# Single-bank gate and up products, and state-space scan blocks with one exponential, summed feature-major by TensorE

## The chip, the cores and the metric

The kernel runs on one core of a Trainium2 chip as one launch. The metric is the device time in microseconds (us), taken as the median of three runs, and lower is better. Engines are named as in the profile: PE is TensorE's matmul (PEld its weight load), DVE is VectorE, ACT is ScalarE, POOL is GpSimd, and SP is the queue that issues most of the DMAs.

## What is computed

Two layers of an encoder over 1024 tokens of width 1024. Each layer has one input projection, four mixers (latent attention "mla", a long convolution "hyena", windowed attention "swa", a state-space scan "ssd"), a norm and an output projection, a gated feed-forward, and a gated per-layer embedding. The change touches the scan and the first half of the feed-forward. Cut to those:

```python
D_MODEL = 1024; SEQ = 1024; D_FF = 2816; SSD_HEADS = 4; SSD_HEAD_DIM = 64; SSD_GROUPS = 2; SSD_CHUNK = 128
...
    a_cs = jnp.cumsum(A, axis=-1)
    seg = a_cs[..., :, None] - a_cs[..., None, :]
    lmat = jnp.exp(jnp.where(tril, seg, -jnp.inf))
    cb = jnp.einsum('bctgn,bcsgn->bgcts', Cc, Bc)
    y_diag = jnp.einsum('bgcts,bgrcts,bcsgrp->bctgrp', cb, lmat, X)
...
    y_off = jnp.einsum('bctgn,cbgrpn,bgrct->bctgrp', Cc, prev, jnp.exp(a_cs))
...
    y = y_f + y_b + dsum * xs            # forward scan, backward scan, skip
...
        y_d = ssd_mixer(...) * jax.nn.silu(ssd_z)
...
        gate = dwconv_centred(h @ ffn_w_gate[i], ffn_conv_w[i], ffn_conv_b[i])
        f = (jax.nn.silu(gate) * (h @ ffn_w_up[i])) @ ffn_w_down[i]
```

## The kernel before

All of a program's engines work from one list of operations. Generators write the list (`interleave` mixes several flows by shares, `stagger` starts a flow's next item one step behind the last), and a scheduler then sets each engine's order by its own simulated timeline, so the order on an engine is not always that of the text. An engine works through its own list in order: an operation that waits holds up all behind it on that engine.

**PSUM.** Results of matmuls land in PSUM, here in two pools: `one()` gives one of four single-bank tiles of 128x512 (named "ps" in the profile), `two()` one of two tiles of two banks, 128x1024 (named "pp"). Together they are eight banks.

**The scan stage.** In each layer `ssd`, `swa` and `mla_keys` are interleaved (402 to 531 us in layer 0 of the profiled execution, 1978 to 2107 us in layer 1). `ssd` cuts the tokens into 8 chunks of 128 and the four heads into 2 groups. `states(c, g)` makes the chunk's state: two transposes, `xt` on ACT, `xd` on DVE, one matmul, and the running `prev`. `output(c, g)`, 16 times in a layer, makes the result: on PE a mask matmul of 512 columns (L880) and 8 matmuls of 128 columns (L885) that put the log decays into one bank; on ACT four exponentials of 128x128, each with its own bias column `lg`, give `Lm`; on PE the two products of C with B and with `prev` into bank `pc`; on DVE `wt` (two steps) and `yo`; on POOL the sum of the two directions of `yo`; on PE a transpose of that sum (L906) and the product of `wt` with `xt`; on ACT a copy `yt` of the transpose; on DVE two additions of 64x128 that write y over B's own buffer (named "xbc<-ps,yt"). After all outputs, z and xs are read from DRAM again, DVE adds `dsum` times xs and DVE and POOL multiply by z (L923 to L927), and y is stored. Seven of the eight "X" buffers of 8 KB per partition are in use by then. `mla_keys` takes four of them for its `kT` in the stage's second half, as the scan gives them back.

**Gate and up.** `gate_up` (about 780 to 1245 us in layer 0, 2350 to 2815 us in layer 1) makes both products of the feed-forward for 22 blocks of 128 features by a two-by-two scheme with 7 products in place of 8. One product is 12 matmuls of 512 columns in one bank: 4 blocks of the inner dimension, times three because an operand is split into a high and a low part (`split`: ACT writes the high part, POOL or DVE the rest, L84 and L87). For a feature the two weights come by DMA into the two `wraw` buffers (`load`, L1372), DVE and POOL form sums and differences (`s`, and `wraw` over itself), five parts are split into the ring "H" of 8, and the products are read out of PSUM by DVE with an addition (to `u`, `v`, `g`) or by ACT (to `v`). Two pairs of products share a two-bank tile: the products with t2 and t1 (`pa`), and those with t4 and 22 (`pb`). The first product of the next features runs in `first`, the convolution and SiLU of a feature in `gated`, and its stores in `paired`. The first features' `first` runs ahead of the loop (`starts`). All these matmuls show as line L99, in `mm`; DVE's and POOL's additions as L87, ACT's work as L84, DVE's multiply-adds as L90.

## Time and profile before

| what | value |
|---|---|
| time, median of 3 runs | 3204.69 us (3196.22 to 3207.54) |
| profiled execution, own time | 3194.46 us |
| its span, first to last instruction | 3192.7 us |
| mean granted clock of TensorE in it | 0.970 |
| busy PE, DVE, POOL, ACT | 2946.4, 2440.4, 1771.2, 1291.6 us |
| as a share of the span | 92%, 76%, 55%, 40% |
| scan stages | 402 to 531 us, 1978 to 2107 us |
| feature loops of gate and up | about 818 to 1245 us, 2385 to 2815 us |

A busy share is time with an instruction at work; matmuls are pipelined and their ends are modelled, so the step from one matmul's start to the next one's start is a better measure of what it costs than its duration. A timeline's row gives start, duration, engine, line, operation, what is written and read, and how many instructions of one kind are put together; in square brackets stand the idle time ahead of it on its engine and what ended it. A granted clock of 1.00 is TensorE's level of 2.4 GHz, and 0.50 that of 1.2 GHz. The profiled execution lies 10.2 us (0.3%) under the median of the runs.

### The profile page before, as it was taken

The page shows a single profiled execution, that of the slowest core. Times are in us where ns is not written, and L with a number is a line of the kernel's source. Part 1 is how long each engine was busy: PE and PEld are TensorE (multiplying, and loading weights), DVE is VectorE, ACT ScalarE, POOL GpSimd, SP SyncE. Part 2 cuts the span into 40 slices and gives each one's busy share as a digit, 9 for nine tenths or more (in the row PEclk, how much of TensorE's full clock was granted, in tenths as well). Part 3 has the DMA queues.
Part 4 walks back from the last instruction along what each step waited for, and adds up shares of the span by engine and source line. Part 5 has one row for each costly group of instructions (what it writes and reads, how often), then busy time and mean ns, then how long its engine had stood idle before and what let it go on. Part 6 is the DMA issues. An engine that isn't in the chain of part 4 may idle for free.

```text
span 3192.7 us, 40546 instructions
## 1 busy us (share of the span) xinstructions
PE 2946.4 (92%) x14316; PEld 2420.9 (76%) x14316; DVE 2440.4 (76%) x3711; ACT 1291.6 (40%) x2278; POOL 1771.2 (55%) x1371
## 2 busy tenths in 40 slices
PE   6999988999899999999989998889989999999996
PEld 4887866877678777787867877768767787777785
DVE  7678786878766777889777786868786677768986
ACT  4332365743333334443342333667333333344341
POOL 5455533527555666887435463335185556679845
PEclk9999998999999999999999998999999999999998
DMA  5466523022233326523335664130322333274332
GB/s 181 152 202 213 180 85 137 16 84 86 76 99 106 102 96 225 189 93 124 114 107 159 219 215 158 53 122 17 107 73 83 99 111 99 101 257 146 106 132 89
DMA packets 153427, 400.44 MB, mean 125 GB/s; under 512 B 16578, under 2 KB 43462, under 8 KB 152968
## 3 DMA queue, kind: packets, MB, share of 16 engines
q1 hardware_dynamic: 138968, 347.18, 32.5%
q0 software_dynamic: 14256, 50.67, 5.2%
q8 instruction: 114, 1.87, 0.2%
q14 instruction: 89, 0.73, 0.1%
HBM read 294.50 MB, written 103.28 MB: 125 GB/s over the span
## 4 chain that ended last, share of the span: by engine, by line
PE 48%; DVE 22%; POOL 9%; DMA 8%; issue 8%; ACT 5%; SPq 0%; DVEq 0%; POOLq 0%; ACTq 0%
PE ps L99 17%; PE pp L99 15%; PE ps L1613 7%; DMA wraw<-in_ffn_w_gate_dram 4%; POOL H L87 2%; DVE g L90 2%; DVE u L87 2%; PE ps L942 2%; DVE w L87 2%; POOL w L87 2%; DVE H L90 2%; PE ps L1054 1%; DVE v L87 1%; ACT w L84 1%; POOL wraw L87 1%
## 5 line engine op out<-in xcount | busy, mean ns | idle before, releaser
L99 PE MATMUL pp<-x,wh 128*128 128x512 f32 x1344 | 430.0, 398 | 1.8 <-ACT wh L84 1.8
L1613 PE MATMUL ps<-part 128*128 128x512 f32 x1440 | 341.4, 393 | 14.7 <-DVE H L87 6.1
L87 POOL TENSOR_TENSOR w<-wraw,w 128x512 fp32r<-128x512 f32 x164 | 232.7, 1431 | 206.0 <-ACT w L84 205.8
L1613 PEld LDWEIGHTS ps<-part 128*128 128x128 f32 x1440 | 270.8, 189 | 78.4 <-DVE H L87 9.8
L99 PEld LDWEIGHTS pp<-x,wh 128*128 128x128 f32 x1344 | 256.1, 193 | 54.2 <-ACT wh L84 2.0
L99 PE MATMUL ps<-x,w 128*128 128x512 f32 x1056 | 261.6, 395 | 10.8 <-ACT v L84 10.8
L99 PE MATMUL pp<-x,w 128*128 128x512 f32 x1056 | 258.3, 394 | 14.1 <-DVE v L87 9.7
L99 PE MATMUL pp<-x,wl 128*128 128x512 f32 x672 | 266.8, 397 | 3.8 <-POOL wl L87 3.8
L99 PE MATMUL pp<-xq,w 128*128 128x512 f32 x1056 | 264.4, 392 | 5.8 <-DVE x L87 4.5
L84 ACT ACTIVATE w<-wraw 128x512 fp32r<-128x512 f32 x264 | 152.8, 622 | 267.6 <-DMA wraw<-in_ffn_w_up_dram 169.9
L87 POOL TENSOR_TENSOR wl<-wraw,wh 128x1024 fp32r<-128x1024 f32 (+2 forms) x61 | 153.6, 2520 | 173.6 <-ACT wh L84 119.8
L99 PEld LDWEIGHTS pp<-x,w 128*128 128x128 f32 x1056 | 196.9, 188 | 63.7 <-DVE v L87 13.8
L87 POOL TENSOR_TENSOR part<-fr,part 128x512 fp32r<-128x512 f32 x140 | 220.5, 1602 | 43.7 <-ACT part L84 43.4
L99 PEld LDWEIGHTS ps<-x,w 128*128 128x128 f32 x1056 | 199.0, 190 | 59.9 <-ACT v L84 18.0
L99 PEld LDWEIGHTS pp<-xq,w 128*128 128x128 f32 x1056 | 198.0, 188 | 51.2 <-ACT w L84 5.1
L99 PE MATMUL ps<-wo,yn 128*128 128x512 f32 x768 | 188.0, 401 | 5.5 <-DVE H L90 3.1
L87 DVE TENSOR_TENSOR part<-wr,part 128x512 fp32r<-128x512 f32 x124 | 155.5, 1278 | 39.0 <-ACT part L84 38.7
L1039 POOL TENSOR_TENSOR P<-P,smr 128x1024 f32<-128x1024 f32 x64 | 121.2, 1895 | 110.1 <-DVE smr L1038 101.2
L99 PEld LDWEIGHTS ps<-wo,yn 128*128 128x128 f32 x768 | 145.4, 193 | 39.6 <-DVE H L90 5.4
L99 PE MATMUL ps<-wh,x 128*128 128x512 f32 x512 | 158.7, 390 | 0.0
L99 PEld LDWEIGHTS pp<-x,wl 128*128 128x128 f32 x672 | 129.1, 192 | 30.6 <-POOL wl L87 4.7
L90 DVE SCALAR_TENSOR_TENSOR g<-g,pp 128x1023 f32<-128x1023 f32 x88 | 128.4, 1460 | 27.0 <-ACT g L84 25.6
(385 smaller groups left out, 7264.5 us busy)
## 6 DMA issues: line engine op xcount, KB each, us to landing
fr<-fp SPq DMA_DIRECT2D x70, 512.0 KB, 3.7
c_fwd<-in_c_fwd_dram POOLq DMA_DIRECT2D x64, 512.0 KB, 5.4
wraw<-in_ffn_w_up_dram SPq DMA_DIRECT2D x50, 512.0 KB, 3.5
fp<-u SPq DMA_DIRECT2D x100, 256.0 KB, 2.4
wraw<-in_ffn_w_gate_dram SPq DMA_DIRECT2D x44, 512.0 KB, 3.8
wraw<-in_w_in_dram SPq DMA_DIRECT2D x42, 512.0 KB, 3.7
wr<-in_ffn_w_down_dram SPq DMA_DIRECT2D x36, 512.0 KB, 4.8
c_inv<-in_c_inv_dram POOLq DMA_DIRECT2D x32, 512.0 KB, 4.8
```

The lines of the kernel that those rows point to most:

```text
L84: self.nc.scalar.activation(out, in_, func, **kw)
L87: (eng or self.nc.vector).tensor_tensor(out, a, b, op=op)
L90: return self.nc.vector.scalar_tensor_tensor(out, a, s, b, op0=op0, op1=op1)
L99: ins = self.nc.tensor.matmul(out, a, b, start=i == 0, stop=i == n - 1)
L942: ins = self.nc.tensor.matmul(out[0:64] if j else out, v[:, 0, :] if j else v.rearrange("p i d -> p (i d)"), terms[i][1 + j], start=k == 0 ...
L1039: nc.gpsimd.tensor_tensor(P, P, sm.to_broadcast([128, T]), op=ALU.mult)
L1054: nc.tensor.transpose(pt[:, j * 128:(j + 1) * 128], P[:, c0:c0 + 128], self.ident)
L1613: nc.tensor.matmul(ps, u, v, start=k == 0 and (p != 1 or ch == 0), stop=k == 5 and (p != 1 or ch == last))
```

## The change

Gate and up: around the feature loop the pool of two-bank tiles is closed and a pool of four single-bank tiles ("pt") opened in its place (`swap2`), and products go in turn to "pt" and "ps", so a product never shares a tile; at the loop's end the pool is set back. The scan: `lg` is split in two parts (`lgs`), and two matmuls of 512 columns add it to the log decays in PSUM, so that one exponential of 128x512 without a bias makes all of `Lm`. The skip term becomes a matmul of xs with a diagonal matrix (`skip`), the `wt` product is made as two halves of 64 columns, and the two directions of `yo` are added by two matmuls with the identity, all into the same 128 columns of `py`. DVE's one last step multiplies that by z and writes y. For that z is read into an eighth X buffer, `zs`, as the stage begins. The POOL sum, the transpose, the ACT copy, the two additions, the second reading of xs and z and the last passes over all of y go away.

```diff
+    def swap2(self, name, bufs):
+
+        self.st2.close()
+        self.ps2 = self.st2.enter_context(self.tc.tile_pool(name=name, bufs=bufs, space=PSUM, reuse_waits="tile"))
 
...
+        zs = self.xp.tile([128, 2, T], F32, name="zs", tag="X")
+        for g in range(2):
+            nc.sync.dma_start(zs[:, g], zd[:, g])
+        sk = self.pool(ss, f"sk{l}")
+        skip = sk.tile([128, 2, 128], F32, name="skip")
+        for g in range(2):
+            self.act(skip[:, g], self.ident, scale=dsum[:, g:g + 1])
+        lgs = [sk.tile([128, 8, 8], F32R, name=f"lg{i}") for i in range(2)]
+        self.split(*lgs, lg)
...
+            for a in lgs:
+                nc.tensor.matmul(bv, self.identr, jv(a, c, g, 128), start=False, stop=False)
             for d in range(2):
                 for h in range(2):
                     j = d * 4 + g * 2 + h
@@ -885,10 +903,7 @@
                         nc.tensor.matmul(bv[:, d, h, :], a[:, c, j:j + 1].to_broadcast([128, 128]), self.tri[:, d, :],
                                          start=False, stop=a is Al and d + h == 2)
             yield
-            for d in range(2):
-                for h in range(2):
-                    j = d * 4 + g * 2 + h
-                    self.act(Lm[:, d, h, :], bv[:, d, h, :], AF.Exp, bias=lg[:, c, j:j + 1])
+            self.act(Lm, bv, AF.Exp)
...
-            yo = s2.tile([128, 2, 2, 64], F32, name="yo", bufs=3)
-            self.tt(yo, pc[:, 256:512].rearrange("p (d h x) -> p d h x", d=2, h=2), jv(eacs, c, g, 64), ALU.mult)
+            yo = s2.tile([128, 2, 128], F32, name="yo", bufs=3)
+            self.tt(yo.rearrange("p d (h x) -> p d h x", h=2), pc[:, 256:512].rearrange("p (d h x) -> p d h x", d=2, h=2),
+                    jv(eacs, c, g, 64), ALU.mult)
             self.tt(wt, wt, pc[:, 0:128].unsqueeze(1).to_broadcast([128, 2, 128]), ALU.mult)
             yield
-            self.tt(yo[:, 0], yo[:, 0], yo[:, 1], ALU.add, nc.gpsimd)
-            yield
-            py = self.one()
-            nc.tensor.transpose(py[:, 256:384], yo[:, 0].rearrange("p h x -> p (h x)"), self.ident)
-            yield
-            yt = s2.tile([128, 128], F32, name="yt", bufs=3)
-            self.act(yt, py[:, 256:384])
-            self.mm(py[:, 0:256], [(xt[g][:, c, 0], wt.rearrange("p h t -> p (h t)"))])
-            yield
-            y = res[1, g]
+
+            py = self.one()[:, 0:128]
+            nc.tensor.matmul(py, skip[:, g], res[0, g][:, cs], start=True, stop=False)
             for h in range(2):
                 hs = slice(h * 64, h * 64 + 64)
-                self.tt(y[hs, cs], py[hs, h * 128:h * 128 + 128], yt[hs], ALU.add)
+                nc.tensor.matmul(py[hs], xt[g][:, c, 0, hs], wt[:, h], start=False, stop=False)
+            for d in range(2):
+                nc.tensor.matmul(py, yo[:, d], self.ident, start=False, stop=d == 1)
+            yield
+            self.tt(res[1, g][:, cs], py, zs[:, g, cs], ALU.mult)
...
-        for g in range(2):
-            nc.sync.dma_start(res[2, g], zd[:, g, :])
-            x = self.wp.tile([128, T], F32, name="wraw", tag="wraw", bufs=2)
-            nc.sync.dma_start(x, xbc[0][:, g])
-            self.stt(res[1, g], x, dsum[:, g:g + 1], res[1, g], ALU.mult, ALU.add)
-            self.tt(res[1, g], res[1, g], res[2, g], ALU.mult, nc.gpsimd if g else nc.vector)
-        yield
...
-            def product(w, b, ps=None):
-                ps = self.one() if ps is None else ps
+            def product(w, b):
+                if next(turn):
+                    ps = self.ps2.tile([128, 512], F32, name="pt", tag="pt")
+                else:
+                    ps = self.one()
...
-                lo, hi = slice(0, 512), slice(512, 1024)
-                pa = self.two()
                 u = small()
-                self.tt(u, product(w2, B["t2"], pa[:, lo]), v1, add)
+                self.tt(u, product(w2, B["t2"]), v1, add)
                 u4 = small()
-                self.tt(u4, product(w1, B["t1"], pa[:, hi]), u, add)
+                self.tt(u4, product(w1, B["t1"]), u, add)
...
-                pb = self.two()
-                self.tt(g[:, 0:512], product(w22, B["t4"], pb[:, lo]), u, add)
+                self.tt(g[:, 0:512], product(w22, B["t4"]), u, add)
                 c12 = fu.tile([128, 512], F32, name="u", tag="u", bufs=6)
-                self.tt(c12, product(w4, B["22"], pb[:, hi]), u4, add)
+                self.tt(c12, product(w4, B["22"]), u4, add)
...
+            turn = itertools.repeat(0)
...
+            turn = itertools.cycle((1, 0))
+            self.swap2(f"ps3_{l}", 4)
             for f in range(NF):
                 last = feature(f, last, starts[f] if f < 3 else None)
             gated(*last)
...
```

On PE, in layer 0's feature loop, the first matmul of each product of one feature before (x_7021 and x_7023 are the operands of `first` and its second step, xq_7624, x_7622, xq_7626, xq_7628 and x_7620 those of t2, t1, t3, t4 and 22):

```order
L99 MATMUL pp_9169<-xq_7624,w2_9156 128x512 [waits DVE_49]
L99 MATMUL pp_9095<-x_7620,w2_9022 128x512 [waits DVE_49]
L99 MATMUL ps_9359<-xq_7626,w2_9308 128x512 [waits Activation_49]
L99 MATMUL pp_9169<-x_7622,w2_9151 128x512 [waits DVE_49]
L99 MATMUL pp_9244<-xq_7628,w2_9162 128x512 [waits DVE_49]
L99 MATMUL ps_9374<-x_7023,w2_9295 128x512 [waits DVE_49]
L99 MATMUL ps_9425<-x_7021,w2_9422 128x512 [waits Activation_49]
```

and after (x_6993 and x_6995, then xq_7596, x_7594, xq_7598, xq_7600 and x_7592 in the same roles):

```order
L100 MATMUL pt_9911<-xq_7596,w2_9897 128x512 [waits Activation_49]
L100 MATMUL ps_9926<-x_7594,w2_9892 128x512 [waits DVE_49]
L100 MATMUL pt_9952<-xq_7598,w2_9900 128x512 [waits DVE_49]
L100 MATMUL ps_9967<-x_6995,w2_9887 128x512 [waits DVE_49]
L100 MATMUL pt_9981<-xq_7600,w2_9903 128x512 [waits DVE_49,Activation_49]
L100 MATMUL ps_9996<-x_7592,w2_9907 128x512 [waits DVE_49,Activation_49]
L100 MATMUL pt_10019<-x_6993,w2_10016 128x512 [waits DVE_49,Activation_49]
```

Before, the halves of a tile stand apart, with products of the neighbouring feature and of "ps" between them; after, a feature's products stand in the order of the text, one bank each, and a bank comes up again eight products later.

On PE, in the scan stage of layer 0, from one output to the next before:

```order
L906 MATMUL ps_4464<-ident_116,yo_4370 128x128 [waits PE_49,Activation_49,Pool_49]
L99 MATMUL ps_4414<-wt_4306,xt_3562 128x256 [waits Activation_49]
L99 MATMUL ps_4470<-xbc_3555,xbc_3552 128x128 [waits PE_49,Activation_49]
L99 MATMUL ps_4470<-prev_3563,xbc_3555 128x256
L99 MATMUL ps_4464<-wt_4347,xt_3562 128x256 [waits Activation_49]
L880 MATMUL ps_4479<-mask_130,identr_132 128x512 [waits DVE_49,PE_49]
L885 MATMUL ps_4479<-tri_128,s_Ah_612 128x128
```

and after:

```order
L921 MATMUL ps_4469<-xbc_3549,skip_3571 128x128 [waits Activation_49]
L924 MATMUL ps_4469<-wt_4388,xt_3564 64x128 x2
L926 MATMUL ps_4469<-ident_116,yo_4427 128x128 x2
L100 MATMUL ps_4478<-xbc_3555,xbc_3552 128x128 [waits DVE_49]
L100 MATMUL ps_4478<-prev_3563,xbc_3555 128x256
L896 MATMUL ps_4484<-mask_130,identr_132 128x512 [waits DVE_49,PE_49]
L898 MATMUL ps_4484<-lg0_3574,identr_132 128x512
L898 MATMUL ps_4484<-lg1_3575,identr_132 128x512
L903 MATMUL ps_4484<-tri_128,s_Ah_612 128x128
```

An output's last part, two pieces before with POOL and ACT between them, is one piece after, with three waiting matmuls in a round in place of four.

On SP, as the scan stage begins, before:

```order
L612 DMA z0_271<-cv_3476 128x1024 [waits DMAHW6_49,Activation_49]
L826 DMA xbc_3549<-xs0_276 128x1024 [waits DMAHW7_49,PE_49]
L826 DMA xbc_3555<-cs0_278 128x1024 [waits DMAHW4_49]
L1105 DMA wraw_4249<-sk0_273 64x1024 [waits DMAHW5_49,DVE_49]
L612 DMA z0_271<-cv_3534 128x1024 [waits DMAHW7_49,Activation_49]
L1108 DMA wraw_4254<-sq0_272 128x1024 [waits DMAHW0_49,PE_49]
```

and after:

```order
L619 DMA z0_271<-cv_3476 128x1024 [waits DMAHW5_49,Activation_49]
L833 DMA xbc_3549<-xs0_276 128x1024 [waits DMAHW7_49,PE_49]
L833 DMA xbc_3555<-cs0_278 128x1024 [waits DMAHW4_49]
L842 DMA zs_3565<-z0_271 128x1024 [waits DMAHW5_49,PE_49]
L1111 DMA wraw_4262<-sk0_273 64x1024 [waits DMAHW6_49,DVE_49]
L1114 DMA wraw_4267<-sq0_272 128x1024 [waits DMAHW0_49,PE_49]
L619 DMA z0_271<-cv_3534 128x1024 [waits DMAHW1_49,Activation_49]
L842 DMA zs_3565<-z0_271 128x1024 [waits DMAHW2_49,DMAHW1_49]
```

The two halves of z, 512 KB each, are read in here, the first ahead of swa's keys; rows of the same load are left out.

## Rows read from the trace of the kernel before

**Rows 1.** Windows, gate and up, layer 0: PE, PEld, DVE, ACT, POOL busy, clock, DMA, GB/s.

```profile
835.00:1235.00 400.00, 389.33 (x1683) 314.34 (x1682) 293.56 (x326) 139.03 (x205) 230.81 (x163) 1.00 0.33 108
```

**Rows 2.** Waits of PE, feature loop of layer 0: total us, times, longest.

```profile
PE pp L99 <- DVE v L87: 4.8, 4, 1.6
...
PE pp L99 <- DVE g L87: 2.3, 3, 1.3
```

**Rows 3.** Waits of PE, feature loop of layer 1, the longest sum.

```profile
PE pp L99 <- DVE v L87: 5.4, 5, 1.6
```

**Rows 4.** Timeline of all engines, layer 0, around one wait of PE.

```profile
1137.26 2.89 PE L99 MATMUL ps<-x,w 128*128 128x512 f32 x12
...
1139.99 2.91 PE L99 MATMUL pp<-xq,w 128*128 128x512 f32 x12
...
1142.89 0.69 DVE L87 TENSOR_TENSOR s<-wraw 128x512 f32<-128x512 f32 x1 [3.01 <-DMA wraw<-in_ffn_w_gate_dram]
...
1144.24 3.03 PE L99 MATMUL pp<-x,w 128*128 128x512 f32 x12 [1.34 <-DVE g L87]
...
1144.38 1.57 POOL L87 TENSOR_TENSOR w<-s,w 128x512 fp32r<-128x512 f32 x1 [1.66 <-ACT w L84]
...
1147.11 2.91 PE L99 MATMUL ps<-xq,w 128*128 128x512 f32 x12
```

**Rows 5.** Windows, the scan stage of both layers, and 22 us of layer 0's.

```profile
402.00:531.00 129.00, 112.56 (x621) 86.85 (x622) 97.71 (x325) 81.43 (x249) 44.99 (x45) 0.93 0.23 70
1978.00:2107.00 129.00, 110.86 (x619) 84.82 (x619) 96.97 (x325) 81.94 (x250) 44.98 (x46) 0.93 0.24 73
479.00:501.00 22.00, 20.46 (x113) 17.48 (x114) 14.11 (x37) 9.10 (x35) 6.00 (x9) 0.84 0.21 67
```

**Rows 6.** Waits of PE, scan stage of layer 0.

```profile
PE ps L99 <- DVE xd L87: 8.8, 4, 3.8
PE ps L99 <- DVE xbc L87: 2.0, 1, 2.0
PE ps L99 <- ACT Lm L84: 1.5, 3, 0.7
```

**Rows 7.** Timeline of PE, scan stage of layer 1, two outputs.

```profile
2061.22 0.49 PE L99 MATMUL ps<-xbc 128*128 128x128 f32 x2 [0.72 <-ACT Lm L84]
...
2061.55 0.60 PE L99 MATMUL ps<-prev,xbc 128*128 128x256 f32 x2
...
2061.98 0.59 PE L99 MATMUL ps<-wt,xt 128*128 128x256 f32 x2
...
2062.23 0.58 PE L880 MATMUL ps<-mask,identr 128*128 128x512 f32 x1
...
2062.65 0.22 PE L885 MATMUL ps<-tri,s_Ah 128*128 128x128 f32 x1
...
2063.49 0.30 PE L906 MATMUL ps<-ident,yo 128*128 128x128 f32 x1
...
2066.89 0.49 PE L99 MATMUL ps<-xbc 128*128 128x128 f32 x2 [0.67 <-ACT Lm L84]
```

**Rows 8.** Groups by form, scan stage of layer 0: busy us, mean ns, idle before.

```profile
L84 ACT ACTIVATE Lm<-ps,s_lg 128x128 f32<-128x128 f32 x64 | 18.3, 368 | 16.3 <-PE ps L885 16.3
...
L87 DVE TENSOR_TENSOR xbc<-ps,yt 64x128 f32<-64x128 f32 x32 | 9.1, 286 | 1.7 <-PE ps L99 1.3
```

**Rows 9.** Timeline of PE, scan stage of layer 0, around 64-column products.

```profile
516.97 0.40 PE L99 MATMUL ps<-wh,ck 128*128 128x512 f32 x1
517.30 1.51 PE L99 MATMUL ps<-wpt,sV 128*64 128x256 f32 x6
518.74 0.88 PE L1149 MATMUL pp<-ident,ws 128*128 128x128 f32 x6
519.45 0.60 PE L99 MATMUL ps<-wt,xt 128*128 128x256 f32 x2
```

**Rows 10.** Timeline of PE, end of layer 0's scan stage.

```profile
535.06 0.69 PE L99 MATMUL ps<-wh,cn 128*128 128x384 f32 x1 [3.60 <-ACT cn L84]
```

More of the change, by code (lines that the diff above doesn't have):

```diff
@@ L1 @@
+import itertools
 import math
@@ L231, in build @@
         self.ps1 = self.pool(ctx, "ps1", 4, space=PSUM)
-        self.ps2 = self.pool(ctx, "ps2", 2, space=PSUM)
+        self.st2 = ctx.enter_context(ExitStack())
+        self.ps2 = self.pool(self.st2, "ps2", 2, space=PSUM)
         self.dram = self.pool(ctx, "dram", 1, space=DRAM)
@@ L1490, in gate_up @@
             gated(*last)
+            self.swap2(f"ps2_{l}", 2)
     def down(self, l, fd, hmid, H, end, ed):
```

## The prediction

> **What bounds the kernel now.** I began with the busy shares in the table: PE is at work for 92% of the span and no other engine passes 76%, so a stage is shorter only where PE waits less or computes less. The windows over the two stages that the diff touches come next. In gate and up PE is busy 389.33 of 400 us at a granted clock of 1.00, DVE 293.56, POOL 230.81 [rows 1]: PE's own stage, with at most 10.7 us to be had from 400 in each layer. The list of PE's waits says who holds it: DVE, by reading a product of a two-bank tile to `v` (4.8 us in 4 waits) or `g` (2.3 us in 3) [rows 2]; in layer 1 the reading to `v` alone is 5.4 us in 5 waits [rows 3].
>
> The timeline shows how such a wait comes about [rows 4]. DVE stands until 1142.89 for the gate weight's DMA (idle 3.01 us), makes `s`, and only then reads the finished product to `g`; PE, whose next product goes to the other half of that tile, starts it at 1144.24 after 1.34 us of idling. Two products follow each other by 2.73 us when nothing stalls (1137.26 to 1139.99), by 2.87 behind a wait (1144.24 to 1147.11), so a wait costs 0.14 us more than its length.
>
> In the scan stage PE is busy 112.56 of 129 us in layer 0 and 110.86 in layer 1, at a mean clock of 0.93 [rows 5]. Its waits there are mostly for `xd` (8.8 us in 4), which DVE makes late because its buffer waits for DMAs as the stage begins; 2.0 us is for the last addition of y ("xbc"), and 1.5 us for `Lm` [rows 6].
>
> **Gate and up, part by part.** The change removes no product; it gives each its own bank and lets a bank rest for seven products. What it can remove are the waits for a half tile's reader: 4.8 + 2.3 in layer 0 [rows 2], 5.4 [rows 3] plus an estimated 2.3 for `g` in layer 1, 14.8 us in all in some 15 waits, and 15 x 0.14 = 2.1 us of refill: 17 us. Not all comes back, since the operands are nearly as late. In the example the next product's operand, `w` from `s`, is finished by POOL at 1144.38 + 1.57 = 1145.95 [rows 4]. Without the wait PE would have asked for it at 1147.11 - 1.34 = 1145.77, so 0.18 of 1.34 us would stay, about a seventh. I take 15 us of 17. The ends are nothing, if DMA and splits set the pace at once, and 2 x 10.7 = 21 us, the whole idle time. Before the loop the pool change waits for the last two-bank tiles' readers, and after it `down` waits for the last products' readers; I cost both at zero, since such a reading is one DVE step of 0.68 us and half the banks are not affected, and keep 2 us a layer as the upper end (each change can expose one wait like the 1.34 us and its refill).
>
> **The scan, part by part.** Steps between starts give PE's prices [rows 7]. A 256-column product in full precision takes 0.43 us (2061.55 to 2061.98), so one of 128 columns 0.22. The mask matmul of 512 columns takes 2062.65 - (2061.98 + 0.43) = 0.24. The eight decay matmuls take 0.84 (2062.65 to 2063.49), and by their step a one-pass transpose of 128 columns about 0.11. An output gains two 512-column matmuls (0.48) and the skip product (0.22), and two identity products replace one transpose (0.43 - 0.11 = 0.32); the two halves of the `wt` product cost what the whole did. That is 1.02 us, 16.3 us for the 16 outputs of a layer, on the engine that is the bound. The 64-column halves add a change of shape. Around six products of 64 columns, from 516.97 to 519.45, PE takes 2.48 us [rows 9] where 0.23 + 6 x 0.23 + 6 x 0.11 = 2.27 would do: 0.2 for going in and out, 3.4 us a layer for 16 pairs. Its lower end is nothing, if the gap was a load of weights that the new order hides. One rule of the Trainium skill speaks against the change here: "TensorEngine Tiling (Array Packing)", Key Properties, says that a change of tiling mode drains TensorE. The 0.2 us of the row fits it but doesn't prove it; without the rule the sum for PE would be 16.3 us a layer, with it 19.7.
>
> What the change takes away is hops. ACT's four exponentials of 368 ns [rows 8] become one; PE's wait for `Lm`, 0.72 and 0.67 us in every second output of layer 1's example [rows 7], 1.5 us listed in layer 0, should go, and with it the 2.0 us for "xbc" [rows 6], as DVE's two additions of 286 ns become one step and the POOL sum and ACT copy disappear. That is 3.5 us a layer, at PE's price. Of the rest of PE's idling, 16.4 us [rows 5] less 8.8 for `xd` and 3.5 = 4.1 us can be filled with the added work where DVE was the slower engine, since DVE loses half of its 9.1 us of additions [rows 8] and its last passes over y. The `xd` wait I leave as it is: z's 1 MB is read when the DMAs are busiest, against which `xd` stands later in DVE's order; bounds plus 3 and minus 3 us (its longest wait is 3.8 [rows 6]).
>
> Two more terms are on the gain side. In 22 us of layer 0's stage the granted clock was 0.84, worth 0.16 x 22 = 3.5 us of full speed [rows 5]; with fewer waits PE may keep it, and I take 2 us, bounds 0 and 3.5. At the stage's end PE stood 3.60 us for `cn`, that is for a reload of cq [rows 10]; the reloads of xs that held the `wraw` buffers are gone, so part of the added time falls into this wait: I take 2 us, bounds 0 and 3.6. A layer then costs 19.7 - 3.5 - 4.1 - 2 - 2 = 8 us at the full price of the shape changes; I take half of these (1.7 us), as half of the outputs run beside other PE work that changes shape anyway: 6.4, and 5 us after a discount for outputs that fall into DVE-bound stretches. Both layers: plus 10 us.
>
> **The sum.** Minus 15 and plus 10 is minus 5 us on the profiled execution's 3194.46 us, a difference that I put on the median of the runs, 10.2 us higher: 3204.69 - 5, taken as 3199 us. A difference of 0.5% (16 us) is about what a measurement of this kernel can tell from no change.
>
> **The rivals.**
> *The scan pays the full price (slower).* The added work lies on PE's path everywhere and the hops stay as long under other names: the outputs, one every 2.84 us before (two from 2061.22 to 2066.89 [rows 7]), come every 2.84 + 1.02 + 0.2 = 4.06 us. For: PE is 87% busy in the stage [rows 5]. Against: 3.5 us of hops should go. Price 19.7 a layer, 39 us, less 15: plus 24, 3229 us. It ends slower than before by over 16 us once the scan costs 15.5 us a layer.
> *Operands take over in gate and up.* PE, no longer held by banks, is held by the weights: the load lands as late, `s` waits as long, and the splits follow. For: the 0.18 us above, and DVE's 3.01 us for the DMA [rows 4]. Against: DVE and POOL have a quarter and more of the window free [rows 1]. Gain 3 us in place of 15: 3204.69 - 3 + 10 = 3212 us. The change would then not do what it says.
> *Both pay.* Gate and up gives back its 21 us of idling, and the scan ends level, since hops, clock and the wait for cq hide all of the added work: 3184 us; if the scan gains 5 us a layer, 3174. For: DVE, not PE, was late for `xd`, and POOL and ACT leave the chain. Against: PE's share.
>
> **How the numbers follow.** The forecast has 0.44 (3190 to 3209 by its own bounds), the full price 0.13, operands 0.18, both pay 0.25. The predicted time is 3199 us. The range from 3175 to 3222 leaves out the lower end of "both pay" and the upper half of "full price", about one in ten each. Faster by over 0.5% (under 3188.7 us): most of "both pay" and a tenth of the forecast, 0.28. Slower by over 0.5% (over 3220.7 us): two thirds of "full price" and a little of "operands", 0.12. Within: 0.60.
>
> **What would show it.** In the profile after, PE's waits for DVE `v` and `g` in the feature loop should be near zero, the window of 400 us at 396 busy or more, and the loop some 7 us shorter in each layer; waits of PE for ACT, POOL or DVE `w` of several us there would be the operands. In the scan, waits for `Lm` and "xbc" should be gone, `xd` still be there, a stretch of outputs alone should take 3.4 us an output (2.84 less half of the 0.72 + 0.67 of waiting, plus 1.22), and the stage be 3 to 7 us longer. I am wrong if the stage is longer by over 15 us, or shorter at all, or if the feature loop keeps its length.

## The result

The changed kernel takes 3256.4 us (median of 4 runs, 3253.69 to 3260.3) against 3205.6 us for the kernel before, measured beside it: a ratio of 1.0165 with a 95% interval of 1.0143 to 1.0188: 51 us slower by the medians, 53 by the ratio. The profiled execution has a span of 3254.5 us and a mean granted clock of 0.965.

The first step is to see where the two traces part. The table gives, for both layers, marks read off the timelines: the scan stage from the last matmul of the stage ahead to the first of `mla`'s query transposes; the feature loop from its first product with an "xq" operand to the end of its last product; the spacing of the gate weights' loads, (last issue - first issue) / 21; how long before the loop's end the last gate weight was issued; and the way out, from the loop's end to the end of the paired down products.

| layer 0 / layer 1, us | before | changed |
|---|---|---|
| scan stage | 138.2 / 134.9 | 143.7 / 139.8 |
| feature loop | 431.2 / 431.3 | 438.2 / 444.0 |
| spacing of the loads, per feature | 19.72 / 19.73 | 20.62 / 20.87 |
| last load ahead of the loop's end | 45.8 / 45.8 | 34.0 / 34.7 |
| way out | 199.4 / 199.3 | 212.6 / 211.3 |

The scan costs 5 us a layer more, about as forecast. The feature loop, where 15 us were to come back, costs 7 and 13 us more, and the way out of it 13 and 12 us. So 45 of the 55 us that these rows sum to lie in gate and up and behind it (the two profiled spans differ by 61.8 us).

In the window over 400 us of the loop (the columns are those of [rows 1]; the second row is layer 1), TensorE idles longer: it is busy for 13 us less than the 389.33 of before, at an unchanged clock in layer 0.

```profile
848.00:1248.00 400.00, 376.64 (x1613) 301.28 (x1612) 279.36 (x304) 130.77 (x193) 240.85 (x154) 1.00 0.29 94
...
2450.00:2850.00 400.00, 374.89 (x1587) 299.75 (x1587) 273.15 (x299) 127.96 (x189) 238.27 (x152) 0.98 0.28 94
```

PE's waits in layer 1's loop, from 2430 to 2840 us (total, times, longest; they answer to [rows 2, 3]):

```profile
PE ps L100 <- ACT w L85: 13.5, 7, 3.0
PE ps L100 <- DVE u L88: 5.2, 5, 1.1
PE pt L100 <- DVE v L88: 2.0, 5, 0.4
```

The waits for `v` have shrunk, from 5.4 us with a longest of 1.6 to 2.0 with a longest of 0.4. In their place stand 5.2 us for `u`, also a reading of a product by DVE, and 13.5 us that the list puts down to `w`, a part of a weight being split. The timeline of the changed kernel shows what the longest of these was (start, duration, engine, line, operation; in brackets the idle time ahead and what ended it):

```profile
2731.85 2.88 PE L100 MATMUL ps<-x,w 128*128 128x512 f32 x12
...
2738.99 2.13 POOL L88 TENSOR_TENSOR wraw<-wraw 128x512 f32<-128x512 f32 x1
...
2743.57 1.06 ACT L85 ACTIVATE g<-g 128x1024 f32<-128x1024 f32 x1 [2.99 <-DVE g L91]
...
2744.53 1.14 ACT L85 ACTIVATE w<-wraw 128x512 fp32r<-128x512 f32 x2
...
2744.70 1.81 POOL L88 TENSOR_TENSOR u<-u,g 128x512 f32<-128x512 f32 x1 [3.58 <-ACT g L85]
...
2746.47 3.02 POOL L88 TENSOR_TENSOR w<-wraw,w 128x512 fp32r<-128x512 f32 x2
...
2748.78 0.37 SPq L1378 DMA_DIRECT2D wraw<-in_ffn_w_up_dram  x1
...
2749.51 0.33 SPq L1378 DMA_DIRECT2D wraw<-in_ffn_w_gate_dram  x1
...
2755.75 1.26 DVE L88 TENSOR_TENSOR s<-wraw 128x512 f32<-128x512 f32 x1 [5.43 <-DMA wraw<-in_ffn_w_gate_dram]
...
2756.93 0.68 DVE L88 TENSOR_TENSOR u<-ps,v 128x512 f32<-128x512 f32 x1
...
2757.05 0.63 ACT L85 ACTIVATE w<-s 128x512 fp32r<-128x512 f32 x1 [1.40 <-DVE s L88]
...
2757.76 3.75 PE L100 MATMUL ps<-xq,w 128*128 128x512 f32 x8 [3.02 <-ACT w L85]
```

Read it from its second row. POOL is done with the differences of a feature's weights at 2738.99 + 2.13 = 2741.12. What is left of these weights are two splits, one part on ACT and one on POOL, and then the two load buffers are free. But on ACT the SiLU of an earlier feature ("g<-g") comes first in the order, and it waits 2.99 us for the convolution on DVE; on POOL that feature's multiplication ("u<-u,g") comes first and waits 3.58 us for the SiLU. So the two splits start on POOL at 2746.47 and end at 2749.49, and the next gate weight is issued at 2749.51. It is there when DVE makes `s` at 2755.75, having idled 5.43 us for it. Only then does DVE come to the reading "u<-ps,v", 2756.93 to 2757.61, and TensorE, idle for 3.02 us, begins at 2757.76.

That reading is what TensorE waited for, and not the split of `s` to which the list puts it down because it ended last (2757.68). The product that begins at 2757.76 is that of t4. Its own weight part, w22, was split on ACT at 2744.53 and on POOL by 2749.49, 8 us earlier; `s` feeds a product of a later feature. But the four "ps" banks go round, and the bank that is due is that of the product begun at 2731.85, which had been finished for 22 us and had yet to be read to `u`. The program's own list agrees: this product waits for ACT's split of w22 and for that reading. The same holds for every wait listed as `w` in the two loops: w22 had been split some 10 us before, and the reading "u<-ps,v" ends 0.15 us ahead of the product. So in both loops, 24 and 25 us of idling, TensorE waits for DVE to read a bank, as it did before [rows 4], and DVE is late because it stands in its own order for the gate weight. The longest waits cost more than their length in layer 1: from 2755 to 2765 us the granted clock was 0.66, and the product begun at 2757.76 took 5.25 us to the next one's start, where 2.73 is the rule here.

How long DVE stood for the gate weight, in 390 us of layer 0's loop before (845 to 1235 us), in the changed kernel (the same) and in *gate_ord* below (835 to 1225 us):

```profile
DVE s L87 <- DMA wraw<-in_ffn_w_gate_dram: 48.8, 17, 4.3
```

```profile
DVE s L88 <- DMA wraw<-in_ffn_w_gate_dram: 59.8, 18, 4.4
```

```profile
DVE s L88 <- DMA wraw<-in_ffn_w_gate_dram: 19.4, 12, 3.0
```

Nothing in the text put the multiplication ahead of the splits. The scheduler did, since its own timeline changed with the banks. On POOL, for one feature before (the first row is the split of w22, the last that of w4):

```
w2_9162<-wraw_9125,w2_9162
u_8965<-u_8965,g_9054
w2_9166<-wraw_9123,w2_9166
```

and after, from the program's order:

```
wraw_9270<-wraw_9270
u_9104<-u_9104,g_9195
w2_9309<-wraw_9272,w2_9309
w2_9313<-wraw_9270,w2_9313
```

Before, the multiplication stood between the two splits in 22 of 44 features, behind both in 10 and ahead of both in 8; now it stands ahead of both in 36. On ACT little moved: the SiLU stood ahead of both splits in 30 features before, and in 36 now.

The way out of the loop, PE in layer 0 of the changed kernel:

```profile
1262.27 2.91 PE L100 MATMUL ps<-x,w 128*128 128x512 f32 x12
1268.11 7.34 PE L1623 MATMUL pp<-part 128*128 128x512 f32 x24 [2.93 <-DVE v L88]
1278.40 5.56 PE L1623 MATMUL ps<-part 128*128 128x512 f32 x16 [2.95 <-ACT part L85]
1288.60 3.26 PE L1623 MATMUL ps<-part 128*128 128x512 f32 x8 [4.64 <-DVE part L88]
1292.57 25.06 PE L1623 MATMUL ps<-part 128*128 128x512 f32 x102 [0.71 <-DVE H L91]
```

The loop ends at 1265.2, and the first long row of down products starts at 1292.57, 27 us later (before: 1245.0 and 1258.1, with one of the partial products already done). The down weights are the cause: the second pair of them ("wr") is issued 6.5 us behind the loop's end and split at 1277.71, where before it was issued at 1237.90, 7 us ahead of it.

```profile
1271.69 0.90 SPq L1586 DMA_DIRECT2D wr<-in_ffn_w_down_dram  x2
...
1277.71 0.63 ACT L85 ACTIVATE part<-wr 128x512 fp32r<-128x512 f32 x1 [7.22 <-DMA wr<-in_ffn_w_down_dram]
```

### The profile page after: what moved, and what is told of

Read it like the earlier page. It is cut to its first block, busy times and chain, and to the rows that moved or that the text cites. A ratio compares the mean times of both kernels' runs of the same rounds, so it can differ in the third digit from the quotient of the medians.

```text
span 3254.5 us, 41010 instructions
## 1 busy us (share of the span) xinstructions
PE 2995.5 (92%) x14604; PEld 2459.8 (76%) x14604; DVE 2439.8 (75%) x3675; ACT 1271.1 (39%) x2156; POOL 1799.0 (55%) x1337
## 5 line engine op out<-in xcount | busy, mean ns | idle before, releaser
L1623 PE MATMUL ps<-part 128*128 128x512 f32 x1440 | 346.4, 398 | 21.2 <-DVE part L88 8.4
L100 PE MATMUL ps<-x,w 128*128 128x512 f32 x1176 | 287.8, 395 | 20.1 <-DVE u L88 13.2
L100 PEld LDWEIGHTS ps<-x,w 128*128 128x128 f32 x1176 | 221.8, 190 | 74.0 <-issue 18.4
L100 PE MATMUL pt<-x,w 128*128 128x512 f32 x936 | 227.8, 392 | 2.7 <-DVE u L88 2.6
L100 PE MATMUL ps<-xq,w 128*128 128x512 f32 x744 | 189.4, 405 | 27.9 <-ACT w L85 27.9
L100 PE MATMUL pt<-xq,w 128*128 128x512 f32 x840 | 205.1, 393 | 5.2 <-DVE v L88 4.9
L100 PEld LDWEIGHTS pt<-x,w 128*128 128x128 f32 x936 | 175.9, 189 | 44.2 <-ACT v L85 6.4
L100 PEld LDWEIGHTS ps<-xq,w 128*128 128x128 f32 x744 | 142.3, 194 | 66.3 <-ACT w L85 34.2
L100 PEld LDWEIGHTS pt<-xq,w 128*128 128x128 f32 x840 | 156.6, 188 | 44.9 <-DVE v L88 11.6
```

The lines of the kernel that those rows point to most:

```text
L100: ins = self.nc.tensor.matmul(out, a, b, start=i == 0, stop=i == n - 1)
L1623: nc.tensor.matmul(ps, u, v, start=k == 0 and (p != 1 or ch == 0), stop=k == 5 and (p != 1 or ch == last))
```

## The experiments

Theory A: the loss is in the order on ACT and POOL that the scheduler chose for the single banks; the banks themselves are worth what was forecast. Theory B: TensorE's own new order or the banks cost the time. For the scan: TensorE has room for part of the added work and pays the rest.

**Each part alone.** *gate_only* is the changed kernel with `ssd` of the kernel before.

```diff
 gate_up: as changed (swap2, turn, product without ps)
 ssd: as before
```

> The feed-forward's part of the change alone: the scan is that of the kernel before. Theory A (order): the two traces put some 45 of the 52 us into the gate and up loop and the way out of it, so this kernel should take 40 to 48 us more than before (ratio 1.012 to 1.015), the weights' loads 21.6 us apart per feature in layer 1 as in the changed kernel (19.7 before). Rival (scan): if the loss sat in the scan and only showed later, this kernel would be within 10 us of before.

Measured: 3239.05 us, ratio 1.0119 (1.0099 to 1.0140), 38 us more than before; loop 438.2 / 441.7, loads 20.66 / 20.79 apart (not the 21.6 expected, which the changed kernel does not have by this mark either), way out 210.7 / 210.9. The feed-forward's part carries most of the loss, a little less than the 40 to 48 expected.

*ssd_only* is the other half.

```diff
 ssd: as changed (zs, skip, lgs, one Exp, py)
 gate_up: as before
```

> The scan's part of the change alone: gate and up are those of the kernel before. By the shift between the two traces across the scan stage (4.9 us in layer 0, 3.5 us in layer 1) it should take 5 to 12 us more than before (ratio 1.002 to 1.004). If the scan's full price on TensorE counts (19.7 us a layer), 39 us more.

Measured: 3216.78 us, ratio 1.0049 (1.0032 to 1.0066), 13 to 16 us more. The interval reaches from 10 to 21 us, so a little over the 5 to 12 expected. Together the halves give 1.0168, the changed kernel 1.0165: they add up.

**The order put right.** *gate_ord* is gate_only with two edges for each feature: the SiLU and the multiplication of an earlier feature are queued behind the split of the newest feature's w4, on ACT and on POOL. TensorE's order stays that of gate_only, instruction for instruction. The scheduler moves other work along with the edges, though: 192 of DVE's 3714 instructions and 80 of SP's 934 stand elsewhere than in gate_only, so what is measured is the edges with what follows from them in its order.

```diff
+                for i, j in zip(late, behind):       # late: SiLU, multiplication; behind: the two halves of the split
+                    self.tc.add_manual_dep(i, j.name, NoSync, reason="issue_after")
...
-                self.act(tg, tg, AF.Silu)
+                silu = nc.scalar.activation(tg, tg, AF.Silu).ins
...
+                late[:] = [silu, mul]
```

> The feed-forward's part alone, with two order edges per feature: the SiLU of an earlier feature on ACT and its multiplication on POOL are queued behind the split of the newest feature's last weight part (w4); TensorE's order is that of gate_only. Theory A (the weights come late since SiLU and multiplication stand ahead of the last two splits on ACT and POOL, so the load buffers come free late): loads 19.2 to 20.2 us apart, PE's waits for w under 5 us a layer, time between 12 us less and 10 us more than before. Theory B (the loss is in TensorE's strict order or in the single banks): as gate_only, 40 to 48 us more than before.

Measured: 3156.16 us, ratio 0.9849 (0.9824 to 0.9874), 47 us less than before and 83 less than gate_only. That is far more than the expectation of 12 us less to 10 more allowed, and the loads, 18.4 us apart, come faster than the 19.2 to 20.2 expected. In the windows of its two loops TensorE has no idle time at all:

```profile
835.00:1225.00 390.00, 390.00 (x1710) 320.79 (x1709) 308.14 (x331) 143.62 (x206) 256.56 (x165) 1.00 0.35 119
...
2395.00:2780.00 385.00, 385.00 (x1688) 316.66 (x1687) 311.06 (x327) 141.56 (x204) 256.21 (x165) 1.00 0.35 120
```

No wait of PE is listed in either. The loop takes 405.6 / 405.5 us, and 148 products of 2.73 us are 404. The same place in its timeline as above, with the SiLU and the multiplication now behind the splits:

```profile
2654.22 1.87 POOL L1387 TENSOR_TENSOR w<-wraw,w 128x512 fp32r<-128x512 f32 x1 [3.38 <-ACT w L1386]
...
2656.12 0.33 SPq L1379 DMA_DIRECT2D wraw<-in_ffn_w_up_dram  x1
...
2656.32 0.63 ACT L1386 ACTIVATE w<-wraw 128x512 fp32r<-128x512 f32 x1 [2.17 <-PE ps L100]
...
2656.86 1.04 ACT L1450 ACTIVATE g<-g 128x1024 f32<-128x1024 f32 x1
...
2657.03 1.31 POOL L1387 TENSOR_TENSOR w<-wraw,w 128x512 fp32r<-128x512 f32 x1 [0.93 <-ACT w L1386]
...
2658.30 1.74 POOL L1453 TENSOR_TENSOR u<-u,g 128x512 f32<-128x512 f32 x1
...
2658.37 0.33 SPq L1379 DMA_DIRECT2D wraw<-in_ffn_w_gate_dram  x1
```

ACT's last split stands at 2656.32, the SiLU behind it at 2656.86; POOL's last split ends at 2657.03 + 1.31 = 2658.34, and the gate weight is issued at 2658.37; the multiplication runs beside the load. Theory B falls: with TensorE's order and the banks of gate_only, the edges turn 36 us more (by the medians) into 47 us less.

*gate_ordp* has the edge on POOL only.

```diff
-                late[:] = [silu, mul]
+                late[:] = [None, mul]
```

> As gate_ord, but only POOL's multiplication is queued behind the last split; ACT's SiLU stays where gate_only has it. Theory A with POOL as the holder: nearly as gate_ord, within 8 us of it. Theory A with ACT as the holder (its high parts of the last two splits stand behind the SiLU, which waits for the convolution on DVE): most of the loss stays, 25 to 45 us more than before. Theory B: as gate_only.

Measured: 3182.45 us, ratio 0.9943 (0.9923 to 0.9963): 57 of the 83 us come from POOL's edge, the rest from ACT's, so neither form of the theory was quite right. The loop is at 409.0 / 411.9, nearly the floor, but the last load is issued only 32.8 us ahead of its end and the way out takes 213.1 / 210.6, as in gate_only. With ACT's edge too the lead is 47.2 us in both layers and the way out 201.2 / 201.5. So in these kernels the way out follows how far the loads run ahead.

**Banks or order.** *before_ord* puts the two edges into the kernel before, with its two-bank tiles.

```diff
 gate_up of the kernel before (two(), pa, pb)
+ the edges of gate_ord
```

> The kernel before with the two order edges of gate_ord (SiLU on ACT and its multiplication on POOL behind the newest feature's last split), two-bank tiles kept. Theory A (both are needed: the banks held TensorE in the kernel before, the order holds it in the changed one): the waits for the other half's reader stay, the loop stays at 420 us or more, time 0 to 15 us less than before. Rival (the order alone is the gain and the banks are worth nothing): the loop comes to about 405 us as in gate_ord, time 40 us or more less than before.

Measured: 3172.97 us, ratio 0.9904 (0.9888 to 0.9921), 31 us less: more than expected, less than the rival. The loop stays at 423.9 / 424.1, as Theory A had it, and the loads come 19.0 us apart, 53 us ahead of the loop's end; the way out is 193.5 / 193.0. But the loop is not long for the reason of Theory A. Away from its two ends the waits for the other half's reader are gone, and it runs as fast as gate_ord's (250 us of layer 1, before_ord and then gate_ord):

```profile
2450.00:2700.00 250.00, 249.69 (x1094) 204.76 (x1093) 181.03 (x213) 87.73 (x131) 145.47 (x106) 1.00 0.33 105
```

```profile
2450.00:2700.00 250.00, 250.00 (x1097) 205.70 (x1096) 207.93 (x219) 92.35 (x134) 166.74 (x109) 1.00 0.33 109
```

So there the order does without the single banks what they were to do. Of the 18 us between the two loops, 9 lie in the first 20 products (64.4 us from the first start to the last in layer 0, where gate_ord takes 55.0) and 5.5 in two products of down that before_ord makes inside its loop, and its way out is 8 us shorter. By the medians gate_ord is 17 us faster; whether that is owed to the single banks or to TensorE's order, which before_ord does not share with it, is open.

*before_late* is the opposite: the kernel before, two-bank tiles, with w22's split queued behind the SiLU and the multiplication, the order that the changed kernel has.

```diff
+                for i, j in zip(late, behind):       # at w22's split
+                    self.tc.add_manual_dep(j, i.name, NoSync, reason="issue_after")
```

> The kernel before, two-bank tiles kept, with the opposite order edges: the high part of the newest feature's w22 on ACT and its low part on POOL are queued behind the SiLU and the multiplication of an earlier feature, the order that the changed kernel has. Theory A (this order by itself makes the loads late): loads 20.6 us or more apart, loop 438 us or more, 25 to 50 us more than before. Rival (the order hurts only with single banks): within 10 us of before.

Measured: 3266.21 us, ratio 1.0207 (1.0185 to 1.0228), 66 us more, where 25 to 50 were expected. The order costs more with two-bank tiles than the changed kernel lost; so with readings this late, a bank that comes up only eight products later seems to hide part of the cost. The loads are 21.2 us apart, but here they are not late, 47 us ahead of the loop's end. What PE waits for, from 840 to 1243 us of layer 0's loop of 464.8 us, are the two-bank tiles again:

```profile
PE pp L99 <- DVE g L87: 19.2, 17, 3.7
PE pp L99 <- DVE v L87: 17.0, 11, 2.9
```

So the same order does its harm through the same kind of wait, a reading by DVE that comes late, of a shared tile here and of a single bank in the changed kernel. DVE stands 60.0 us for the gate weight here, from 845 to 1235 us, close to the 59.8 of the changed kernel; what share of the lateness is owed to that was not followed up, and the scheduler also placed other work anew.

*gate_swap* asks what the way out owes to closing the pool: the two-bank pool is opened again ahead of the last feature.

```diff
             for f in range(NF):
+                if f == NF - 1:
+                    turn = itertools.repeat(0)
+                    self.swap2(f"ps2_{l}", 2)
                 last = feature(f, last, starts[f] if f < 3 else None)
             gated(*last)
-            self.swap2(f"ps2_{l}", 2)
```

> gate_ord with the pool of two-bank tiles opened again ahead of the last feature, whose products all go to the four tiles of one(). If the way out of the loop (200 us from the last product to the end of the paired down products in gate_ord, 193 in before_ord) is held by the wait for single-bank tiles, it comes back to 193 to 196 and the time is 6 to 14 us under gate_ord's. If the down products' operands hold it, it stays at 200 and the time is within 4 us of gate_ord's, or more by the last feature's waits for banks.

Measured: 3152.79 us, ratio 0.9852 (0.9829 to 0.9874): the same as gate_ord within the intervals, with a way out of 200.6 / 200.2 us. And gate_ord's way out had shown that no wait for the pool was left, PE in layer 0:

```profile
1224.24 2.91 PE L100 MATMUL ps<-x,w 128*128 128x512 f32 x12
1226.99 5.60 PE L1633 MATMUL pp<-part 128*128 128x512 f32 x24
1232.43 3.79 PE L1633 MATMUL ps<-part 128*128 128x512 f32 x16
1240.31 3.78 PE L1633 MATMUL ps<-part 128*128 128x512 f32 x8 [4.10 <-DVE part L88]
1244.27 6.10 PE L1633 MATMUL ps<-part 128*128 128x512 f32 x22 [0.18 <-DVE H L91]
```

The first down products begin at 1226.99, 2.75 us behind the last product's start, without a wait; the 4.10 us are for an operand of DVE. The 2.93 us for `v` in the changed kernel were DVE being behind with its readings, not a price of the pool.

**The scan's two halves.** *ssd_exp* takes the single exponential alone, *ssd_sum* the sums on TensorE with z read early.

```diff
 ssd_exp: + lgs, + two matmuls of 512 columns, one Exp; the rest as before
 ssd_sum: + zs, skip, py on TensorE; four Exp with a bias as before
```

> The scan's single exponential alone: two matmuls of 512 columns more per output, one ACT step in place of four; POOL sum, transpose, copy, additions and last passes as before. TensorE gains 0.48 x 16 = 7.7 us a layer and loses the waits for Lm (1.5 to 2.1 us): 0 to 12 us more than before, 6 expected. Rival (ACT's chain of four exponentials was the stage's bound): 3 us or more less than before.

> The scan's sums by TensorE alone, with z read at the start: skip product, halves of 64 columns, two identity products, one DVE step; four exponentials as before. TensorE gains 0.54 x 16 = 8.6 us a layer and up to 3.4 us for the changes of shape, and loses the wait for the last addition (2.0 us): 4 to 18 us more than before, 10 expected. With ssd_exp it should add up to ssd_only (13 to 16 us). Rival (the shorter chain on POOL, ACT and DVE pays for it): no more than before.

Measured: ssd_exp 3199.34 us, ratio 0.9991 (0.9979 to 1.0003); ssd_sum 3200.3 us, ratio 0.9993 (0.9982 to 1.0004). Neither costs anything that 12 and 11 runs can tell, where 6 and 10 us were expected, and they do not add up to ssd_only's 13 to 16 us. Four windows, each from the first exponential of layer 0's scan to the last (PE, PEld, DVE, ACT, POOL busy, then the clock), show why; before, ssd_exp, ssd_sum, ssd_only in turn:

```profile
435.00:503.00 68.00, 60.00 (x346) 48.82 (x346) 52.39 (x167) 39.75 (x136) 25.21 (x27) 0.92 0.18 55
```

```profile
440.00:510.00 70.00, 64.97 (x379) 52.80 (x378) 52.13 (x166) 31.31 (x89) 25.45 (x27) 0.95 0.18 54
```

```profile
440.00:509.00 69.00, 66.91 (x443) 54.23 (x443) 46.86 (x162) 38.53 (x125) 14.99 (x12) 0.98 0.15 46
```

```profile
447.00:520.00 73.00, 71.18 (x474) 58.85 (x473) 47.20 (x162) 29.37 (x78) 14.34 (x12) 1.00 0.14 44
```

PE idles 8.0 of 68 us before, 5.0 of 70 with one half, 2.1 of 69 with the other, 1.8 of 73 with both. Either half fits into the idling, and both do not. To separate this from shapes and waits, *ssd_pad* adds TensorE's part of the exponential's edit to ssd_sum, and *ssd_lite* takes work out of ssd_only and leaves its terms out of the result.

```diff
 ssd_pad:  ssd_sum, + two matmuls of 512 columns per output that add zeros
 ssd_lite: ssd_only, - the second matmul of lgs, - the identity product of yo[:, 0]
```

> ssd_sum with two more matmuls of 512 columns per output that add zeros to the log decays; the four exponentials stay. Saturation: TensorE's 0.48 x 16 = 7.7 us a layer come at nearly full price on top of ssd_sum, 8 to 16 us more than before. Rival (the two halves disturb each other through ACT's single step, not through TensorE's time): within 4 us of ssd_sum's time.

> ssd_only without the second matmul of lg (its low part) and without the identity product of the first direction of yo, both left out of the result: 0.46 us less of TensorE's work per output, 7.4 us a layer; the changes of shape and the waits are those of ssd_only. Saturation: 8 to 15 us less than ssd_only, so 0 to 6 us more than before. Rival (changes of shape or waits make ssd_only's cost): within 4 us of ssd_only, 12 to 16 us more than before.

Measured: ssd_pad 3211.88 us, ratio 1.0028 (1.0016 to 1.0040), 9 us more than before and 11 to 12 more than ssd_sum; ssd_lite 3204.62 us, ratio 1.0005 (0.9993 to 1.0018), 2 us more than before and some 12 less than ssd_only. Both as saturation has it: once TensorE is full, 15 us of its work cost 11 to 14. The changes of shape and the waits, which ssd_lite keeps, can be no large part of what ssd_only pays.

**Put together.** *after_ord* is the whole changed kernel with the edges; *best_exp* and *best_sum* are gate_ord with one half of the scan's change.

```diff
 after_ord: changed kernel + the edges of gate_ord
 best_exp:  gate_ord + ssd_exp
 best_sum:  gate_ord + ssd_sum
```

> The whole changed kernel with the two order edges of gate_ord. If the parts add up: gate_ord's 47 us less plus ssd_only's 13 to 16 us more, so 28 to 36 us less than before (3168 to 3176 us, ratio 0.989 to 0.991). Rival (scan and feed-forward hide each other's cost): within 6 us of gate_ord.

> gate_ord with the single exponential of ssd_exp. ssd_exp alone was 3 us under before, ssd_only, which has the sums on TensorE too, 13 to 16 us over it. If TensorE has room for one of the two edits but not for both, this is 0 to 5 us under gate_ord. If edits of the scan cost more once the feed-forward is faster, 5 us or more over it.

> gate_ord with TensorE's sums of ssd_sum, four exponentials as before. By ssd_sum's 2 us under before: 0 to 5 us under gate_ord. If the eighth X buffer or the early reading of z costs something later, over it.

Measured: after_ord 3166.97 us, ratio 0.9885 (0.9868 to 0.9901), a little better than the sum of its parts; best_exp 3150.21, 0.9839 (0.9814 to 0.9864); best_sum 3147.26, 0.9834 (0.9814 to 0.9854). These two and gate_ord can't be told apart by their intervals; all three beat both kernels, and the change as it was written would have been 1.15% faster than before with two order edges. A third load buffer, the other way to take away the late release, is not among the runs.

## Why the prediction was wrong

**What bounds the kernel, and what the banks free.** Right in that TensorE's idling in the loop is to be had: where nothing holds it the loop comes to 405.5 us, 26 us a layer less than before (2.7 of them for a down product that the loop before includes). The 17 us for both layers that I summed from the listed waits [rows 2, 3] were too few: once the order is right TensorE does not idle at all, so the window's 10.7 us a layer [rows 1] were a better bound, and even that counts as busy the restarts that a modelled end hides. But here the prediction failed first, at "what it can remove are the waits for a half tile's reader". I put these waits down to the sharing of a tile. They are for DVE, which is late with its readings behind the gate weight [rows 4]: with a bank for each product and later loads TensorE idled 24 and 25 us in the two loops for such readings, and with shared tiles and earlier loads (before_ord) these waits went away in the loop's middle.

**What stays of it.** Here the prediction failed again. I said that the operands are nearly as late, and sized that from one example as a seventh of the gain, 0.18 of 1.34 us [rows 4], with "nothing" as the lower end. The example was misread: the product begun at 1147.11 is that of t3, whose weight part was split on ACT by 1130.41, and the `w` from `s` that POOL ends at 1145.95 feeds a later product. And the step took ACT's, POOL's and DVE's work to run in the order of the trace of before. It doesn't: their order is set by the same scheduler from the same new program. The rival "operands take over" was right that the load lands late and `s` waits, and wrong that TensorE is then held by the weights; and its price (3 us of gain left) had the same fault, since it could not turn into a loss. The `w` waits that I named as its sign did appear in the list, but stand for readings. The runs put 35 to 38 us more in its place (gate_only), and 83 us between the two orders with the same banks. The order was there to read ahead of the run: I looked at TensorE's and SP's rows and not at POOL's, where the multiplication had moved ahead of two splits in 36 features, from 8.

**The way out of the loop.** I cost the change of pools at zero with 2 us a layer as the end. As for the pools that was right (gate_swap). The way out still took 12 to 13 us more, by late down weights, which I had not looked at: the loads' lead of 45 us at the loop's end is what hid them, and it fell to 34.

**The scan.** The mechanism was right and the size short: plus 10 us forecast, 13 to 16 measured (10 to 21 by the interval), and 5 us a layer forecast between the marks, 5.5 and 4.9 in the changed kernel's trace. The waits for `Lm` and "xbc" [rows 6] are gone from the list, PE is busy throughout the stage's second half (windows of layer 0, columns as [rows 5]):

```profile
459.00:479.00 20.00, 20.00 (x133) 16.71 (x131) 16.72 (x67) 10.84 (x35) 6.93 (x5) 1.00 0.05 12
479.00:501.00 22.00, 22.00 (x164) 19.31 (x163) 12.19 (x40) 5.46 (x12) 1.90 (x2) 1.00 0.07 25
501.00:514.00 13.00, 13.00 (x87) 11.04 (x87) 6.16 (x21) 4.68 (x11) 0.80 (x1) 1.00 0.05 21
514.00:531.00 17.00, 17.00 (x110) 12.59 (x109) 9.69 (x31) 9.52 (x26) 2.88 (x6) 1.00 0.10 28
```

and the clock stayed at 1.00 where it was 0.84 [rows 5]; that term was right in kind. I was wrong on `xd`, which I left as it is: 1.0 us where 8.8 were, with a wait for POOL in its place.

```profile
PE pp L1155 <- POOL ws L1149: 4.3, 1, 4.3
PE ps L100 <- DVE wyt L1164: 1.8, 1, 1.8
PE ps L862 <- DMA xbc<-xs: 1.5, 1, 1.5
PE ps L100 <- DVE xd L88: 1.0, 3, 0.5
PE ps L100 <- ACT cn L85: 0.9, 1, 0.9
```

The row for `cn`, 0.9 us in place of 3.60 [rows 10], fits that part of the added time went into that wait, as forecast. What I called a discount for idling is the larger part of it: TensorE had 8 us to give in layer 0's window, and either half of the scan's change cost nothing that the runs could tell. The price of the changes of shape, 0.2 us a pair from [rows 9], is not settled by itself. The rule of the Trainium skill ("TensorEngine Tiling (Array Packing)", Key Properties: a change of tiling mode drains TensorE) is neither shown nor refuted here. PE's busy time from mark to mark rose by 11.8 and 12.7 us a layer in ssd_only, less than the 16.3 us without any such price; part of the added work may stand in gaps that the modelled ends had counted as busy, and at the higher clock the rest takes less.

**The rivals and the chances.** "The scan pays the full price" ended nearest to the measured time (3229 us), still 27 us under it, and for the wrong reason; the scan did not pay it. "Both pay" was the nearest to what gate and up can give, and needed another order than the scheduler's. No rival had a loss in gate and up, so the range ended at 3222 us.

## What to carry to other kernels

Where a scheduler sets the order, an edit that frees one resource changes the order on engines that it does not touch: read the new order of every engine on the operand path, above all what now stands ahead of the instructions that free a load buffer. A gain read as "PE waits for X" holds only if X was the cause: ask why the engine that is waited for is late, and whether the change makes it earlier; two order edges (NoSync, which order without a semaphore) were worth 83 us here, more than five times the 15 us that I had put on the banks. Where a product waits for two engines, the list names the one that ended last, so look up whether that one feeds the product at all. And idle time of the busiest engine is a budget: two edits that are free alone may cost in full together, so they are measured apart and together.

## What was not expected of the hardware

TensorE can be kept without any idle time over 385 and 390 us (gate_ord) at a granted clock of 1.00 while products go in turn to eight banks and DVE and ACT read them. And in the four windows of the scan above the granted clock was 0.92, 0.95, 0.98 and 1.00, in the order of TensorE's busy share (60.00 of 68 us to 71.18 of 73): so a part of the added work may have been given back that way. That the one made the other was not tested.
